# Second group of the first half's output contraction and the gate's second products, placed between the last chunk and the last heads' turns

## The chip, the cores and the metric

The kernel runs on one core of a Trainium2 chip. The metric is the device time of one execution in microseconds. TensorE is PE here, VectorE DVE, ScalarE ACT, GpSimd POOL; SP is the engine whose queue issues most loads.

## The reference, cut to what matters

Two layers over a sequence of 512 tokens with 1024 features. Layer 0 is an RWKV-7 time mixing with a SwiGLU FFN, layer 1 a differential attention with a SwiGLU FFN. The change lies at the end of the time mixing:

```python
_, y = lax.scan(step, state0, (r, decay, k, v, a, b))      # per head, 16 heads of 64
y = (y - mean) * rsqrt(var + LNX_EPS)                       # norm of each head
y = y * lnx_w + lnx_b + bonus
return (y * g) @ w_o                                        # g = sigmoid(xg @ g1) @ g2
...
x = x + rwkv7_time_mix(...)
h = rms_norm(x, g_ffn[0])
x = x + swiglu_ffn(h, w_gu, w_down)
```

## The kernel before, in words

Features lie on partitions, tokens along the free axis; weights and activations of most products are split into a high and a low part, so that one product is three matmuls (`mm3`, L156 to L158: high x high, high x low, low x high). The 16 heads are worked in two halves `w` of 8 heads, and each half's recurrence (`rec`) runs over 8 chunks of 64 tokens.

One chunk (`chunk`) is a chain between PE and DVE: products `L841` with V and the old state, a copy `L850` to SBUF, 16 small products `L855`, a copy `L860`, products `L841` with V and that copy, and the new state (`L868`, `L871`). The outputs of the chunk before (`chunk_y`, two groups of 24 small products `L883`, each copied by ACT in `L884`) are written between them. After two chunks a token tile of 128 is complete, and `head_out` makes its head norm: a first part (`L892` to `L899`, with the square `L896` on ACT), a second part (`L903` to `L914`: loads of V, the bonus on POOL, a root in ten small steps on DVE, the gain) and a third part, the turn to features on partitions: four transposes `L918` on PE and four copies `L921` on ACT into `oT`. `rec` runs these parts one or two chunks behind and drains them at its end.

`out_half(w)` closes a half. Its first step is the gate: `gate2` loads two tables (`g2a` through `L142`, `g2b` in three parts through `L436`), splits them (`L432`, `L433`, `L437`, `L438`) and makes four banks of four matmuls (three of `mm3` and `L443`); each bank is multiplied into `oT` and split (`ev`: `L650`, `L654`, `L656`). Then come two groups `gi` of four output tiles, each over the four feature tiles of the half: eight steps of 4 x 3 = 12 matmuls. Every second step loads 512 KB of `w_o` (`L142`), casts it on ACT (`L670`) and takes the low part on DVE (`L671`). When a group is done, `add` (`L662`) adds its banks to the residual `x1`.

`plan` writes the steps of three streams in an order by due times (`TIMES`): pairs, solve and recurrence of half 0; projections, gate and `out_half(0)`; pairs, solve and recurrence of half 1. A scheduler then orders each engine's queue by what it expects to be ready, and each engine works its queue in that order. So all of `out_half(0)` lies between the chunks of the second recurrence. `out_half(1)` is drained after the plan, behind `turn()`, which hands the space of the state tiles to the FFN. All weights share the tag `wr` with three buffers, for the raw tile and for the low part; PSUM banks are `ca` (2), `cb` (2) and `pj` (4). In the FFN `gain_split` (`L296`, `L297`) needs the finished residual.

Of the kernel before, what the change touches and what calls it, by code (L numbers as in the profile page):

```python
# [9 lines left out]
F32 = mybir.dt.float32  # L10
F32R = mybir.dt.float32r
BF = mybir.dt.bfloat16
AF = mybir.ActivationFunctionType
ALU = mybir.AluOpType
# [4 lines left out]
P = 128  # L19
# [23 lines left out]
class Trunk:  # L43
# [115 lines left out]

    def proj_k(self, W, x, evac, gi=0, banks=("pj",) * 4):  # L160


        pss = [self.bank(t) for t in banks]
        for kt in range(KT):
            if kt % 2 == 0:
                wh, wl = self.load_w(W[gi, kt // 2], [P, 2, 512])
            for i in range(4):
# [5 lines left out]

    def proj_f(self, W, xgen, evac, kts=range(KT), gi=0):

        pss = [self.bank() for _ in range(4)]
        for kt in kts:
            if kt % 2 == 0:
                w = self.load_raw(W[gi, kt // 2], [P, 2, 512])
            x = xgen(kt)  # L180
# [5 lines left out]

    def proj_p(self, W, xgen, evac, gi=0):

        nc = self.nc
        pss = [self.bank() for _ in range(4)]  # L190
        for kt in range(KT):
            if kt % 2 == 0:
                w = self.load_raw(W[gi, kt // 2], [P, 2, 512])
                wz, xz = (self.T("z", [P, 4, 512], F32R) for _ in range(2))
# [228 lines left out]
        nc.scalar.copy(self.low[:, 0, :], t)  # L423
        nc.vector.tensor_tensor(out=self.low[:, 1, :], in0=t, in1=self.low[:, 0, :].bitcast(F32), op=ALU.subtract)

    def gate2(self, pg, w, evac):

        nc, A = self.nc, self.A
        c0 = slice(w * 512, w * 512 + 512)
        raw = self.load_raw(A["g2a"][:, c0], [P, 512])  # L430
        hi, lo, st = (self.T("pr", [P, 512], F32R) for _ in range(3))
        nc.scalar.copy(hi, raw)  # L432
        nc.vector.tensor_tensor(out=lo, in0=raw, in1=hi.bitcast(F32), op=ALU.subtract)  # L433
        raw = self.T("wr", [P, 512])
        for i in range(3):
            nc.sync.dma_start(raw[i * 32:i * 32 + 32], A["g2b"][:, c0])  # L436
        nc.scalar.copy(st[0:96], raw[0:96])  # L437
        nc.vector.tensor_tensor(out=st[32:64], in0=raw[32:64], in1=st[32:64].bitcast(F32), op=ALU.subtract)  # L438
        for i in range(4):
            ps = self.bank()  # L440
            c = slice(i * P, i * P + P)
            self.mm3(ps, hi[:, c], lo[:, c], pg[0], pg[1], True, False)
            nc.tensor.matmul(ps, st[0:96, c], pg[2][0:96], start=False, stop=True)  # L443
            evac(w * 4 + i, ps)

    def rwkv(self, turn):
        nc, A = self.nc, self.A
        xT = self.h
        rstd = self.norm_cols(xT, "pr", True)
        bc = self.rows_bc(rstd, "pr")  # L450
        cp = self.cp
        self.omu = cp.tile([P, 6 * KT], F32, name="omu")
        i0 = VI["mu0"] * KT
        nc.vector.tensor_scalar(self.omu, self.par[:, i0:i0 + 6 * KT], -1.0, 1.0, op0=ALU.mult, op1=ALU.add)
        h = xT

        def normed():
            for j in range(KT):
                v = h[j // 2][:, j % 2, :]
                nc.vector.scalar_tensor_tensor(out=v, in0=v, scalar=self.vec("g_mix0", j), in1=bc, op0=ALU.mult, op1=ALU.mult)  # L460
                yield
        self.h = h
        self.Dc = cp.tile([P, NP, NCH], F32, name="Dc")
        self.bon = cp.tile([P, NT, NP, 2], F32, name="bon")
        self.rkc = cp.tile([P, NP, 2], F32, name="rkc")
        for p in range(NP):
            nc.vector.tensor_scalar(self.rkc[:, p, :], self.cst[:, C_BO:C_BO + 2], self.vec("r_k", p), None, op0=ALU.mult)
        self.lw = cp.tile([P, D], F32, name="lw")
        self.v_d = self.dr.tile([2, 2, S, 4, C], F32, name="v_d")
        self.st_d = self.dr.tile([2, NCH, P, 4, 8 * C], F32, name="st_d")  # L470
        self.sel = cp.tile([P, NT, P], F32, name="sel")
        self.R, self.Pt, self.kept = {}, {}, {}
        self.oT = {}

        self.merge(*zip((normed(), self.lora_h(h, "ca"), self.r_half(0)), self.START))
        sg, aa = self.rates(0)
        kr, ld, pg, sa, x1 = ([], []), ([], []), [], [(sg, aa)], []
        nc.gpsimd.dma_start(self.sel, A["sel"])
        self.drain(self.k_half(0, kr[0]))
        nc.sync.dma_start(self.lw, A["lnx_w"].broadcast_to([P, D]))  # L480

        def rates():
            sa.append(self.rates(1))
            yield

        def out(w):
            if w == 0:
                x1.extend(self.load_x())
            yield from self.out_half(w, pg, x1)
        t = self.TIMES  # L490
        self.plan(
            [(lambda: self.pairs(0, kr[0], *sa[0], ld[0]), 20, *t["pairs0"]), (lambda: self.solve(0, *ld[0]), 36, *t["solve0"]),
             (lambda: self.rec(0), 24, *t["rec0"])],
            [(lambda: self.r_half(1), 8, *t["r1"]), (lambda: self.k_half(1, kr[1]), 8, *t["k1"]), (rates, 1, t["k1"][1], t["k1"][1]),
             (lambda: self.v_half(0), 8, *t["v0"]), (lambda: self.v_half(1), 8, *t["v1"]), (lambda: self.gate(pg), 8, *t["gate"]),
             (lambda: out(0), 9, *t["out0"])],
            [(lambda: self.pairs(1, kr[1], *sa[1], ld[1]), 20, *t["pairs1"]), (lambda: self.solve(1, *ld[1]), 36, *t["solve1"]),
             (lambda: self.rec(1), 24, *t["rec1"])])
        turn()
        self.drain(out(1))  # L500
        return x1

    def mixes(self, key, m, w):
# [107 lines left out]
    def rec(self, w):  # L611
        for i in range(2):
            self.oT[w * 2 + i] = self.T("s", [P, 2, S])
        st, out, prev = None, [], ()
        nxt = self.chunk_load(w, 0)
        for c in range(NCH):
            cur, nxt = nxt, self.chunk_load(w, c + 1) if c < NCH - 1 else None
            if c % 2 == 0:
                y = self.T("ho", [P, 2, 4, C])
            fill = [self.chunk_y(*prev, par) for par in range(2)] if prev else []  # L620
            new, U = yield from self.chunk(w, c, st, *cur, fill)
            if c > 0 and c % 2 == 0:
                out.append(self.head_out(w, c // 2 - 1, prev[-1]))
            for g in out:
                next(g, None)
            out = out[-2:]
            prev = (c, st, U, *cur, y)
            st = new
        for par in range(2):
            next(self.chunk_y(*prev, par))  # L630
        out.append(self.head_out(w, NT - 1, y))
        for g in out:
            self.drain(g)

    def chunk_load(self, w, c):
        z = self.T("z", [P, 4, 8, C])
# [6 lines left out]
    def out_half(self, w, pg, x1):  # L643

        nc, A = self.nc, self.A
        yx, yh, yl = {}, {}, {}

        def ev(o, ps):
            yx[o] = self.T("xk", [P, S])
            nc.vector.tensor_tensor(out=yx[o], in0=ps, in1=self.oT[o // 2][:, o % 2, :], op=ALU.mult)  # L650
            if o % 2 == 0:
                yh[o // 2] = self.T("s", [P, 2, S], F32R)
            h = yh[o // 2][:, o % 2, :]
            nc.scalar.copy(h, yx[o])  # L654
            yl[o] = self.T("xk", [P, S], F32R)
            nc.vector.tensor_tensor(out=yl[o], in0=yx[o], in1=h.bitcast(F32), op=ALU.subtract)  # L656
        self.gate2(pg, w, ev)
        yield

        def add(o, ps):  # L660
            v = x1[o // 2][:, o % 2, :]
            nc.vector.tensor_tensor(out=v, in0=ps, in1=v, op=ALU.add)  # L662
        for gi in range(2):
            pss = [self.bank() for _ in range(4)]
            for kt in range(w * 4, w * 4 + 4):
                k = kt % 2
                if k == 0:
                    W = self.load_raw(A["w_o"][gi, kt // 2], [P, 2, 512])
                    wh, wl = self.T("s", [P, 2, 512], F32R), self.T("wr", [P, 2, 512], F32R)
                    nc.scalar.copy(wh, W)  # L670
                    nc.vector.tensor_tensor(out=wl, in0=W, in1=wh.bitcast(F32), op=ALU.subtract)  # L671
                for i in range(4):
                    c = slice(i * P, i * P + P)
                    self.mm3(pss[i], wh[:, k, c], wl[:, k, c], yh[kt // 2][:, k, :], yl[kt], k == 0 and kt % 4 == 0, kt % 4 == 3)
                    if kt % 4 == 3:
                        add(gi * 4 + i, pss[i])
                yield
# [613 lines left out]
```

## Time and profile before

| | us |
|---|---|
| runs (3) | 1504.1 median, 1504.0 to 1507.41 |
| the profiled execution | 1504.01, span 1502.2, mean granted clock 0.985 |
| PE busy | 1438.6 (96%) |
| DVE, ACT, POOL busy | 775.7, 514.0, 188.6 |
| HBM | 102 GB/s over the span |

A wait is put down to the instruction that came last. Durations of matmuls are modelled at their ends, so the spacing of their starts tells more than the mean of one. The views used are the busy shares, the table by stages, PE's waits, the chain of waits, the timeline, the groups of instructions and the list of loads.

### The profile page before, as it was taken

The numbers are of one execution on the slowest core, as the hardware profiler recorded it, in microseconds if no ns is written. First come the engines' busy times: TensorE is split into PE (matmuls) and PEld (weight loads), VectorE is DVE, ScalarE is ACT, GpSimd is POOL, SyncE is SP. The second block draws the span as 40 slices with busy tenths as digits, with TensorE's granted clock in tenths as the row PEclk, the third lists the DMA queues.
The fourth block names the chain that finished last, engine by engine and source line by source line (L and its number), as shares of the span: only waits on it lengthen the run. The fifth ranks groups of instructions, "written<-read, shape, count | busy, mean of one in ns | idle before, by whom it ended". The sixth has DMA issues, their size and how long they took to land.

```text
span 1502.2 us, 23112 instructions
## 1 busy us (share of the span) xinstructions
PE 1438.6 (96%) x9592; PEld 1142.1 (76%) x9592; DVE 775.7 (52%) x1497; ACT 514.0 (34%) x907; POOL 188.6 (13%) x156
## 2 busy tenths in 40 slices
PE   4999999999996999999999989999999999999998
PEld 2675555766885788888888889988778888888887
DVE  6625559588666643344323376666656444343222
ACT  4633242214323432233212253466654333222111
POOL 0013212101000211111100023110002111111000
PEclk9989999999998999999999999999999999999999
DMA  5203524766311322222222222211012222222231
GB/s 171 80 15 114 184 75 152 281 230 210 134 53 49 121 95 98 97 91 94 98 98 99 98 72 85 85 58 43 29 57 85 98 98 99 98 98 98 98 123 60
DMA packets 56761, 154.76 MB, mean 103 GB/s; under 512 B 10704, under 2 KB 17104, under 8 KB 54608
## 3 DMA queue, kind: packets, MB, share of 16 engines
q1 hardware_dynamic: 55456, 151.71, 29.4%
q8 instruction: 75, 1.23, 0.3%
q10 hardware_dynamic: 1120, 1.32, 0.3%
q14 instruction: 30, 0.25, 0.0%
q0 software_dynamic: 80, 0.26, 0.0%
HBM read 132.29 MB, written 20.97 MB: 102 GB/s over the span
## 4 chain that ended last, share of the span: by engine, by line
PE 83%; DVE 9%; ACT 3%; POOL 2%; issue 2%; DMA 1%; ACTq 0%; POOLq 0%
PE pj L156 15%; PE pj L157 15%; PE pj L158 15%; PE pj L182 3%; PE pj L216 3%; PE d L1067 2%; PE cb L883 2%; PE d L1069 2%; PE d L1068 2%; PE ca L841 2%; PE cb L751 1%; PE a L1165 1%; PE ca L157 1%; PE cb L157 1%; PE ca L156 1%
## 5 line engine op out<-in xcount | busy, mean ns | idle before, releaser
L150 ACT CAST wh<-wr 128x1024 fp32r<-128x1024 f32 x153 | 160.8, 1052 | 498.1 <-PE pj L157 217.5
L151 DVE TENSOR_TENSOR wl<-wr,wh 128x1024 fp32r<-128x1024 f32 x153 | 187.0, 1223 | 184.7 <-ACT wh L150 183.1
L156 PE MATMUL pj<-xa,wh 128*128 128x512 f32 x352 | 139.2, 395 | 1.3 <-ACT wh L150 1.3
L157 PE MATMUL pj<-xa,wh 128*128 128x512 f32 x352 | 138.9, 395 | 0.0
L158 PE MATMUL pj<-xa,wl 128*128 128x512 f32 x352 | 138.8, 395 | 0.0
L156 PE MATMUL pj<-xb,wh 128*128 128x512 f32 x352 | 137.1, 389 | 0.0
L158 PE MATMUL pj<-xb,wl 128*128 128x512 f32 x352 | 137.0, 389 | 0.0
L157 PE MATMUL pj<-xb,wh 128*128 128x512 f32 x352 | 136.9, 389 | 0.0
L954 POOL TENSOR_TENSOR hid<-ev,hid 128x512 fp32r<-128x512 f32 x44 | 68.2, 1551 | 403.6 <-ACT hid L953 403.6
L950 DVE TENSOR_TENSOR ev<-pj,bc 128x512 f32<-128x512 f32 x44 | 30.4, 691 | 144.0 <-PE pj L158 144.0
L947 DVE TENSOR_TENSOR ev<-pj,bc 128x512 f32<-128x512 f32 x44 | 30.4, 692 | 116.6 <-PE pj L158 114.3
L156 PEld LDWEIGHTS pj<-xa,wh 128*128 128x128 f32 x352 | 66.3, 188 | 17.5 <-ACT wh L150 2.2
L158 PEld LDWEIGHTS pj<-xa,wl 128*128 128x128 f32 x352 | 66.3, 188 | 15.6
L157 PEld LDWEIGHTS pj<-xa,wh 128*128 128x128 f32 x352 | 66.3, 188 | 15.2
L157 PEld LDWEIGHTS pj<-xb,wh 128*128 128x128 f32 x352 | 66.1, 188 | 13.8
L156 PEld LDWEIGHTS pj<-xb,wh 128*128 128x128 f32 x352 | 66.1, 188 | 13.7
L158 PEld LDWEIGHTS pj<-xb,wl 128*128 128x128 f32 x352 | 66.1, 188 | 13.5
L158 PE MATMUL pj<-hid,wl 128*128 128x512 f32 x176 | 68.5, 389 | 0.0
L156 PE MATMUL pj<-hid,wh 128*128 128x512 f32 x176 | 68.5, 389 | 0.0
L157 PE MATMUL pj<-hid,wh 128*128 128x512 f32 x176 | 68.5, 389 | 0.0
L216 PE MATMUL pj<-wr,xk 128*128 128x512 f32 x128 | 63.8, 637 | 0.0
L227 POOL TENSOR_TENSOR ty<-ty,mhalf 128x8 f32<-128x8 f32 (+1 forms) x20 | 35.4, 1769 | 156.6 <-DVE ty L1103 125.8
(342 smaller groups left out, 3096.7 us busy)
## 6 DMA issues: line engine op xcount, KB each, us to landing
wr<-in_wgu SPq DMA_DIRECT2D x88, 512.0 KB, 3.5
wr<-in_wdn SPq DMA_DIRECT2D x44, 512.0 KB, 3.5
st_d<-z SPq DMA_DIRECT2D x16, 1024.0 KB, 4.5
z<-st_d SPq DMA_DIRECT2D x16, 1024.0 KB, 5.6
wr<-in_w_kv SPq DMA_DIRECT2D x16, 512.0 KB, 3.6
wr<-in_w_r SPq DMA_DIRECT2D x8, 512.0 KB, 3.5
wr<-in_w_k SPq DMA_DIRECT2D x8, 512.0 KB, 3.4
wr<-in_w_v SPq DMA_DIRECT2D x8, 512.0 KB, 3.7
```

The source lines that it names most:

```text
L150: nc.scalar.copy(hi, raw)
L151: nc.vector.tensor_tensor(out=lo, in0=raw, in1=hi.bitcast(F32), op=ALU.subtract)
L156: mm(out, wh, xh, start=start, stop=False)
L157: mm(out, wh, xl, start=False, stop=False)
L158: mm(out, wl, xh, start=False, stop=stop)
L182: self.nc.tensor.matmul(pss[i], w[:, kt % 2, i * P:i * P + P], x, start=kt == kts[0], stop=kt == kts[-1])
L216: self.nc.tensor.matmul(pss[tt], x[:, tt * P:(tt + 1) * P], w[:, kt % 2, :], start=kt == 0, stop=kt == KT - 1)
L227: nc.gpsimd.tensor_tensor(out=y, in0=m, in1=half.to_broadcast(shp), op=ALU.pow)
L841: nc.tensor.matmul(ps[f, i * C:(i + 1) * C], L(f, i), R[f, i, :], start=False, stop=n == len(parts) - 1 and i == 3)
L947: nc.vector.tensor_tensor(out=a, in0=pss[0], in1=bc, op=ALU.mult)
L950: nc.vector.tensor_tensor(out=b, in0=pss[1], in1=bc, op=ALU.mult)
L954: nc.gpsimd.tensor_tensor(out=t[:, 1, :], in0=b, in1=t[:, 0, :].bitcast(F32), op=ALU.subtract)
```

## The change

Three things move. The second group (`gi` = 1) of `out_half(0)` leaves the plan: the plan now takes five steps of it (the gate and the first group), and the other four are drained after the plan. `rec` no longer drains the last head norm of the second half: its first two parts are written, and the turn is kept as `self.rest`. And `gate2` of the second half is cut in two: its products go to four banks `ca`, `ca`, `cb`, `pj` ahead of that turn, the multiplication `ev` comes after it; ahead of both, the first `w_o` tile of `out_half(1)` is loaded and split (`first`). `gate2` also makes all of its products before the first `ev`, in both halves. `turn()` comes after `out_half(1)`.

```diff
-    def gate2(self, pg, w, evac):
+    def gate2(self, pg, w, evac, banks=("pj",) * 4):
...
-        for i in range(4):
-            ps = self.bank()
+        pss = [self.bank(t) for t in banks]
+        for i, ps in enumerate(pss):
             c = slice(i * P, i * P + P)
             self.mm3(ps, hi[:, c], lo[:, c], pg[0], pg[1], True, False)
             nc.tensor.matmul(ps, st[0:96, c], pg[2][0:96], start=False, stop=True)
+        yield
+        for i, ps in enumerate(pss):
             evac(w * 4 + i, ps)
...
         t = self.TIMES
+        o0 = out(0)
         self.plan(
...
-             (lambda: out(0), 9, *t["out0"])],
+             (lambda: itertools.islice(o0, 5), 5, *t["out0"])],
...
+        o1 = out(1)
+        self.drain(o0)
+        next(o1)
+        self.drain(self.rest)
+        self.drain(o1)
         turn()
-        self.drain(out(1))
...
-        for g in out:
+        for g in out[:-1]:
             self.drain(g)
+        for _ in range(2):
+            next(out[-1])
+        if w:
+            self.rest = out[-1]
+        else:
+            self.drain(out[-1])
...
+        def split(gi, j):
+            W = self.load_raw(A["w_o"][gi, j], [P, 2, 512])
+            wh, wl = self.T("s", [P, 2, 512], F32R), self.T("wr", [P, 2, 512], F32R)
+            nc.scalar.copy(wh, W)
+            nc.vector.tensor_tensor(out=wl, in0=W, in1=wh.bitcast(F32), op=ALU.subtract)
+            return wh, wl
...
-        self.gate2(pg, w, ev)
+        if w:
+            first = split(0, 2)
+            yield from self.gate2(pg, w, ev, ("ca", "ca", "cb", "pj"))
+        else:
+            self.drain(self.gate2(pg, w, ev))
+            first = None
         yield
...
                 if k == 0:
-                    W = self.load_raw(A["w_o"][gi, kt // 2], [P, 2, 512])
-                    wh, wl = self.T("s", [P, 2, 512], F32R), self.T("wr", [P, 2, 512], F32R)
-                    nc.scalar.copy(wh, W)
-                    nc.vector.tensor_tensor(out=wl, in0=W, in1=wh.bitcast(F32), op=ALU.subtract)
+                    wh, wl = first or split(gi, kt // 2)
+                    first = None
```

The changed kernel's statements have other line numbers: `L650` becomes L670, `L654` L674, `L656` L676, `L662` L687, `L670` L664, `L671` L665, `L824` L847, `L841` L864, `L855` L878, `L883` L906, `L912` L935, `L914` L937, `L918` L941. The text goes by those of the kernel before.

On PE between two chunks of the second recurrence (chunk two in the kernel before), what stands between a chunk's last products and the next chunk's first; `pj` banks are the contraction's, `ca` the chunk's. Before:

```order
L841 MATMUL ca_614_3645<-rs_592_3474,z_591_3472 64x64 x8
L157 MATMUL pj_579_3417<-xk_570_3392,s_603_3564 128x512
L841 MATMUL ca_614_3645<-rs_613_3643,z_591_3472 64x64 x8
L158 MATMUL pj_579_3417<-s_566_3380,wr_604_3565 128x512
L156 MATMUL pj_580_3418<-s_566_3380,s_603_3564 128x512
L157 MATMUL pj_580_3418<-xk_570_3392,s_603_3564 128x512
L158 MATMUL pj_580_3418<-s_566_3380,wr_604_3565 128x512
L156 MATMUL pj_581_3419<-s_566_3380,s_603_3564 128x512
L157 MATMUL pj_581_3419<-xk_570_3392,s_603_3564 128x512
L158 MATMUL pj_581_3419<-s_566_3380,wr_604_3565 128x512
```

The same place now:

```order
L847 MATMUL ca_611_3615<-zero_77,cst_63 128x256
L864 MATMUL ca_611_3615<-rs_585_3452,z_584_3450 64x64 x8
L864 MATMUL ca_611_3615<-rs_610_3613,z_584_3450 64x64 x8
L156 MATMUL pj_590_3485<-s_562_3374,s_593_3489 128x512
L157 MATMUL pj_590_3485<-xk_565_3381,s_593_3489 128x512
L158 MATMUL pj_590_3485<-s_562_3374,wr_594_3490 128x512
L156 MATMUL pj_591_3486<-s_562_3374,s_593_3489 128x512
L157 MATMUL pj_591_3486<-xk_565_3381,s_593_3489 128x512
L158 MATMUL pj_591_3486<-s_562_3374,wr_594_3490 128x512
L847 LDWEIGHTS cst_63
L847 MATMUL ca_619_3663<-zero_77,cst_63 128x256
L864 MATMUL ca_619_3663<-rs_603_3552,z_602_3550 64x64 x8
```

Where twelve matmuls of the contraction stood around a chunk's last products, six stand now, and behind two other chunks none.

On PE around the last turn (`L918`, L941 in the changed kernel); `pr` tiles are the gate's table, `pj_732` and `pj_735` the second half's contraction. Before:

```order
L443 MATMUL pj_725_4390<-s_545_3322,pr_716_4360 128x512
L156 MATMUL pj_729_4401<-s_544_3321,pr_714_4358 128x512
L157 MATMUL pj_729_4401<-s_544_3321,pr_714_4358 128x512
L158 MATMUL pj_729_4401<-s_544_3321,pr_715_4359 128x512
L443 MATMUL pj_729_4401<-s_545_3322,pr_716_4360 128x512
L918 MATMUL cb_712_4343<-cst_63,ho_706_4314 128x128 x4
L156 MATMUL pj_732_4411<-s_720_4376,s_737_4417 128x512
```

Now:

```order
L157 MATMUL pj_723_4365<-s_544_3321,pr_716_4351 128x512
L941 MATMUL cb_724_4382<-cst_63,ho_696_4246 128x128 x4
L158 MATMUL ca_720_4362<-s_544_3321,pr_717_4352 128x512
L158 MATMUL ca_721_4363<-s_544_3321,pr_717_4352 128x512
L158 MATMUL cb_722_4364<-s_544_3321,pr_717_4352 128x512
L158 MATMUL pj_723_4365<-s_544_3321,pr_717_4352 128x512
L443 MATMUL ca_720_4362<-s_545_3322,pr_718_4353 128x512
L443 MATMUL ca_721_4363<-s_545_3322,pr_718_4353 128x512
L443 MATMUL cb_722_4364<-s_545_3322,pr_718_4353 128x512
L443 MATMUL pj_723_4365<-s_545_3322,pr_718_4353 128x512
L156 MATMUL pj_735_4413<-s_726_4393,s_713_4345 128x512
```

The 16 gate products stood ahead of the turn; now eight of them (those with the table's high part) and, ahead of these, the moved group of 48 stand before it, and the other eight behind it.

On DVE from the end of the last head norm to the gated tiles. Before:

```order
L908 TENSOR_TENSOR ho_675_4056<-ho_675_4056,ty_709_4324 128x512
L912 TENSOR_TENSOR ho_675_4056<-ho_675_4056,lw_157 128x256 x2
L914 TENSOR_TENSOR ho_706_4314<-ho_675_4056,ho_708_4319 128x4x64 x2
L650 TENSOR_TENSOR xk_719_4374<-pj_718_4369,s_571_3394 128x512
L656 TENSOR_TENSOR xk_721_4378<-xk_719_4374,s_720_4376 128x512
```

Now:

```order
L935 TENSOR_TENSOR ho_668_4006<-ho_668_4006,lw_157 128x256 x2
L937 TENSOR_TENSOR ho_696_4246<-ho_668_4006,ho_698_4251 128x4x64 x2
L687 TENSOR_TENSOR x_550_3335<-pj_702_4275,x_550_3335 128x512
L687 TENSOR_TENSOR x_550_3335<-pj_703_4276,x_550_3335 128x512
L687 TENSOR_TENSOR x_551_3337<-pj_704_4277,x_551_3337 128x512
L687 TENSOR_TENSOR x_551_3337<-pj_705_4278,x_551_3337 128x512
L433 TENSOR_TENSOR pr_717_4352<-wr_715_4349,pr_716_4351 128x512
L438 TENSOR_TENSOR pr_718_4353<-wr_719_4356,pr_718_4353 32x512
L670 TENSOR_TENSOR xk_725_4391<-ca_720_4362,s_571_3394 128x512
```

Four additions of the moved group and two steps of the gate's table have come between the norm's last step and the first gated tile. Further ahead, the split of the early `w_o` tile (`L671`, L665 now) stands among the small steps of the norm's root.

## Rows read from the trace of the kernel before

**Rows 1.** Busy time of PE, with its share of the span and its instructions.

```profile
PE 1438.6 (96%) x9592; PEld 1142.1 (76%) x9592; DVE 775.7 (52%) x1497; ACT 514.0 (34%) x907; POOL 188.6 (13%) x156
```

**Rows 2.** Table by stages: length; busy PE, PEld, DVE, ACT, POOL; clock; DMA share, GB/s.

```profile
470.00:493.00 23.00, 23.00 (x90) 18.46 (x91) 11.31 (x15) 6.32 (x8) 0.00 (x0) 0.89 0.26 91
...
380.00:452.40 72.40, 71.49 (x1074) 60.10 (x1073) 47.70 (x116) 16.98 (x36) 4.69 (x6) 1.00 0.26 86
452.40:469.90 17.50, 5.24 (x24) 3.83 (x23) 10.60 (x28) 5.95 (x14) 1.69 (x2) 0.76 0.14 45
```

**Rows 3.** PE's waits, 380 to 470 us: line waited for, us in total, times, longest.

```profile
PE pj L156 <- ACT s L670: 6.7, 1, 6.7
PE cb L918 <- DVE ho L914: 5.5, 1, 5.5
```

**Rows 4.** Chain of waits from the last chunks to the second contraction: start, us, what.

```profile
438.56 1.40 PE cb L883 x24
440.17 1.08 PE ca L841 x32
...
452.43 0.43 PE pj L157
...
456.10 0.53 ACT ho L896
456.65 0.70 DVE ty L898
...
462.10 1.10 PE cb L918 x4
463.22 1.14 ACT s L921 x4
464.36 0.61 ACT s L654
...
466.32 0.63 ACT s L654
...
469.91 0.79 PE pj L156
```

**Rows 5.** Timeline of PE in the second contraction: start, us, line, tiles.

```profile
475.31 0.40 PE L156 MATMUL pj<-s,s 128*128 128x512 f32 x1
...
478.05 0.39 PE L156 MATMUL pj<-s,s 128*128 128x512 f32 x1
...
492.33 0.39 PE L156 MATMUL pj<-s,s 128*128 128x512 f32 x1
...
494.14 0.39 PE L158 MATMUL pj<-s,wr 128*128 128x512 f32 x1
```

**Rows 6.** Groups of instructions, 376 to 500 us: busy us, mean ns, idle before.

```profile
L662 DVE TENSOR_TENSOR x<-pj,x 128x512 f32<-128x512 f32 x16 | 10.7, 688 | 6.5 <-PE pj L158 6.5
L671 DVE TENSOR_TENSOR wr<-wr,s 128x1024 fp32r<-128x1024 f32 x8 | 9.7, 1216 | 6.7 <-PE pj L158 5.2 <-ACT s L670 1.5
...
L650 DVE TENSOR_TENSOR xk<-pj,s 128x512 f32<-128x512 f32 x8 | 5.5, 685 | 2.3 <-ACT s L921 1.7 <-PE pj L443 0.6
...
L850 DVE COPY rs<-ca 128x256 f32<-128x256 f32 x7 | 2.9, 420 | 4.0 <-PE ca L841 4.0
...
L438 DVE TENSOR_TENSOR pr<-wr,pr 32x512 fp32r<-32x512 f32 x2 | 1.4, 681 | 0.1
...
L437 ACT CAST pr<-wr 96x512 fp32r<-96x512 f32 x2 | 1.2, 616 | 1.1 <-DMA wr<-in_g2b 1.1
```

**Rows 7.** Loads of the page: issues, KB each, median us from issue to landing.

```profile
wr<-in_g2a SPq DMA_DIRECT2D x2, 256.0 KB, 3.0
...
wr<-in_g2b SPq DMA_DIRECT2D x6, 64.0 KB, 2.8
```

**Rows 8.** Table by stages, columns as in rows 2, stretches of small products.

```profile
370.00:375.00 5.00, 4.76 (x27) 1.84 (x25) 4.59 (x17) 3.53 (x5) 0.45 (x1) 1.00 0.33 107
...
437.80:444.40 6.60, 6.60 (x136) 6.00 (x135) 3.57 (x8) 2.03 (x6) 0.34 (x1) 1.00 0.13 41
```

## Prediction

> **What bounds the kernel now.** I read the busy shares first. TensorE (PE) is busy 96% of the span [rows 1], so a change pays only where PE idles or runs at its lower clock; work that is merely moved from one full place to another pays nothing. The table by stages then says where it idles. From 380.0 to 452.4 us, the second recurrence with the first half's output contraction between its chunks, PE works 71.5 of 72.4 us. From 452.4 to 469.9 it works 5.2 of 17.5 us, at a mean granted clock of 0.76. From 470 to 493 it is full again, but at a mean clock of 0.89 [rows 2]. Two waits make nearly all of the hole: 5.5 us for the last `L914` and 6.7 us for the weight cast `L670` [rows 3]. The chain of waits shows what they hang on: the last chunk's `L883` ends at 452.43 (T0 below), then come the head norm on DVE and ACT, the turn `L918` at 462.10, `L921`, and the split of the gated tile (`L650`, `L654`, `L656`). The weight cast `L670` stands in ACT's queue behind the third `L654`, and only after it does the first product of the second half's contraction start, at 469.91 (S below) [rows 4]. S minus T0 is 17.5 us. The hole costs a second time: of the products behind it the first twelve take 5.40 us, from 469.91 to 475.31, about 0.45 each, which is the 1.2 GHz level; at the 2.4 GHz level they follow each other every 0.2267 us (63 steps from 478.05 to 492.33), and twelve take 2.72 [rows 4, 5]. So 2.7 us are lost to the clock. From S to the end of the 96 products (494.14 + 0.23) are 24.5 us.
>
> **The change part by part.** The profiled execution took 1504.01 us with a span of 1502.2; the median of the runs is 1504.1. I count from 1504.0.
>
> *Out of the recurrence.* The second group of the first half is 4 steps of 4 x 3 = 48 products, 48 x 0.2267 = 10.9 us. All of it leaves the stretch in which PE idles 0.9 us of 72.4 [rows 2], so it was on the path, and T0 comes 10.9 us earlier unless PE waits there instead. What it covered are the hand-overs of a chunk: PE ends a product, DVE copies it (`L850`, `L860`, 0.42 us each, or `L868` and `L871`, two such) and PE goes on with the copy. Around each of them the new order still has something: 24 products `L883` of the chunk before (1.40 us), 6 to 7 of the remaining large products, or the half of `L841` that needs no new state. A copy that comes at once (0.42 and some 0.2 for two semaphores) is covered by each of these. It is not where DVE does something else first: in the fourth chunk the copy now stands behind the last wide steps of a head norm (as wide as `L650`, 0.69), in the last behind a weight split `L671` (1.22) [rows 4, 6]. I put 0.3 and 0.4 us for the two. The trace of before has no chunk with so little fill, so the bounds are 0 and 2.4 us (both copies late by one whole `L671`); I stay near the lower end, because the 24 products cover most of either. T0: -10.9 + 0.7 = -10.2 us.
>
> *Into the hole.* After T0 PE's queue now holds 47 of the 48 moved products (10.65 us), the turn of the third token tile (0.55, half of the 1.10 that a turn took at the lower clock), 8 of the gate's 16 products (1.8), and only then the last `L918`: 13.0 us after T0. The head norm is ready before that. It took 9.7 us; `L896` now waits 0.5 us more behind the `L921` of the third tile, and a weight split `L671` (1.2) stands in the middle of its small DVE steps, 11.4 in all. So the norm is hidden and PE's own queue sets the turn. Behind the turn stands the gate: the four `L662` of the moved group, `L433` and `L438` go ahead of the first `L650` on DVE, and `L437` goes behind the last `L921` on ACT. From 13.0: turn 0.55, `L921` 1.14, `L437` 0.62, `L438` 0.68, the first `L443` 0.39, `L650` 0.69, `L654` 0.63, and some 0.5 for the semaphores between them, together 18.2 us after T0, against 17.5 before [rows 4 to 6]. The four `L662` and `L433` (as wide, 0.69) end at 11.4 + 5 x 0.69 = 14.9 and are not last. I take S as 0.8 us later after T0 than it was. The hole does not vanish, it is filled: four waits of 0.5 to 1 us stay in it.
>
> *The loads.* Three slots `wr` serve every weight. The gate's `g2a` can be loaded only when the `L671` of the early split is done: `L898` ends at T0 + 4.9, 0.5 later now, four small steps of 0.2 and the split follow, 7.4; it lands 3.0 us later, its cast (0.61, as `L437`) ends at T0 + 11.1, and PE asks for it at 11.2. `g2b` waits until PE has finished the moved group (T0 + 11.4); its third part is issued 0.9 later and there at 15.1, just when `L437` could read it [rows 4, 7]. I cost both at nothing; if either is late, each us of lateness is a us of the sum. Behind them on the SP queue stands the load of the next `w_o` tile, which is issued some 6 us before S and wanted 4 us after it. The loads of V, state and x stay ahead of these, as they were.
>
> *Second contraction.* Without the long idle time the clock should stay up, which gives back the 2.7 us. Against it: the cast `L670` of the second weight tile still stands behind three `L654`, which come every 1.96 us, so it ends at about S + 5.0, when 18 products (4.1 us) are done [rows 4]. I put 1.4 us for this and for the smaller waits of the next tiles, between 0 and 2.7. Gain 1.3 us.
>
> The sum: -10.2 + 0.8 - 1.3 = -10.7 us, so 1504.0 - 10.7 = **1493.3 us**. After the second contraction the order is as before, and all of it comes 10.7 us earlier.
>
> The Trainium skill, page "TensorE: Matmul & The Clock Gate", section "Back-to-back issue gap", gives about 131 ns as the sustained spacing of matmuls of 512 columns; by it the moved 48 would be 6.3 us and the sum 1497.9, an estimate. The rows show 0.2267 us over 63 steps [rows 5], so the measurement decides and the page's figure enters nothing.
>
> **The rivals.** *The loads come late.* Both gate loads pass through one slot each that is freed late. If that slips by one landing and one cast (3.0 + 0.6) and the recurrence by the rest of its bound (2.4 - 0.7), the sum is -10.7 + 5.3, 1498.6 at most; one of them alone gives 1495 to 1497. For it: both loads meet their reader within 0.2 us by my own count. Against it: landings of this size take about 3 us all through [rows 7].
>
> *The recurrence becomes bound by its hand-overs.* A chunk has three, about 0.6, 0.6 and 1.1 us, 2.3 in all, and seven chunks have them, 16 us. PE waited for hardly any of this before. If what is left covers only a third of it, 10.8 us come back and the change is a wash, 1504. For it: in two places a chunk and a half now pass without a large product. Against it: the groups of 24 products alone cover the first two hand-overs.
>
> *Slower: PE falls to its lower clock in the recurrence.* In those two places PE now has nothing but 64 x 64 products for over 8 us each (four groups `L883` of 1.40 and two and a half `L841` of 1.08) [rows 4]. At 1.2 GHz they would take twice as long, 17 us more, and the time would be 1510; it decides as soon as the granted clock in them reads well under 1.00. Against it: the trace has such a stretch of 6.6 us (437.8 to 444.4) at clock 1.00, and from 370 to 375, with PE's weight loads busy only 1.84 of 5 us, the clock reads 1.00 as well [rows 8]. The same page of the Trainium skill, section "Part 1: The HAM clock gate", says that the throttled state is the default and that activity releases it; no row here shows a recurrence with so few large products, so this keeps a small chance.
>
> That the change does not do what it says is no case of its own: the order shows the 48 products behind the last chunk.
>
> **How the numbers follow.** Forecast 0.75, with 1491 to 1496 of its own; late loads 0.12; bound by hand-overs 0.09; lower clock 0.04. Downward, a gate without waits (S 1 us nearer to T0) and a second contraction without them (1.4) give 1490.9. The range of 1490.5 to 1497.5 holds the forecast and most of the late loads. About 0.3% (4.5 us) is what a measurement here can tell from no change: faster by more than that 0.87, within it 0.09, slower 0.04.
>
> **What would show it.** In the new profile the last `L883` ends near 442.2; the last turn starts about 13 us after it and not 9.7; the wait for `L914` is gone, and small waits for `L433`, `L438` and `L654` stand in its place; the second contraction starts near 460.5, with steps of 0.23 us from the first, and ends near 483.7. The forecast is wrong if PE's waits for `L850`, `L860` and `L871` in the recurrence sum to over 3 us, if `L432` or `L437` waits long for its load, or if the clock reads under 1.00 before S.

## The result and the profile after

The changed kernel takes 1491.7 us (median of 4 runs, 1489.66 to 1492.96) against 1504.78 for the kernel before in the same series: ratio 0.9909, 95% interval [0.9894, 0.9924]. The forecast was 1493.3, range 1490.5 to 1497.5. The profiled execution took 1490.67 us, its span is 1488.9. Line numbers are each kernel's own from here on; in the changed kernel the chunk's products are `L864`, the copies behind them `L873` and `L883` (`L850` and `L860` before), and the second weight cast and split `L664` and `L665`.

PE's busy time, to set beside [rows 1]: 3.5 us less, all of it clock and spacing, since the instructions are the same 9592.

```profile
PE 1435.1 (96%) x9592; PEld 1138.8 (76%) x9592; DVE 774.2 (52%) x1497; ACT 513.9 (35%) x907; POOL 188.3 (13%) x156
```

The table by stages, cut at the same events as [rows 2] (the stretch up to T0, from T0 to S, the second contraction). Columns: stretch; length; busy PE, PEld, DVE, ACT, POOL; granted clock; DMA share, GB/s.

```profile
380.00:440.10 60.10, 59.20 (x1024) 50.14 (x1022) 41.85 (x107) 15.92 (x34) 4.73 (x5) 1.00 0.29 96
440.10:458.10 18.00, 16.11 (x73) 12.47 (x71) 12.36 (x31) 5.94 (x14) 1.85 (x3) 1.00 0.21 69
458.10:481.00 22.90, 22.35 (x95) 17.63 (x96) 14.80 (x21) 8.40 (x13) 0.00 (x0) 1.00 0.25 92
```

The recurrence is 12.3 us shorter, 0.6 of it ahead of its first chunk, and as full as it was (0.9 us idle in both). The hole is 0.5 us longer than it was, but PE now works 16.1 us of it and not 5.2. The clock reads 1.00 in all three, where the last two read 0.76 and 0.89 before.

PE's waits from 378 to 490 us: line waited for, us in total, times, longest. The waits of 5.5 and 6.7 us of [rows 3] are gone; what is left is under 1 us each, but for the first line: `L150` is the FFN's weight cast, and its wait is the same in the kernel before.

```profile
PE pj L156 <- ACT wh L150: 1.3, 2, 1.1
PE ca L864 <- DVE rs L883: 0.8, 1, 0.8
PE ca L443 <- DVE pr L438: 0.8, 1, 0.8
PE pj L156 <- ACT s L674: 0.7, 1, 0.7
PE pj L156 <- ACT s L664: 0.5, 1, 0.5
PE ca L158 <- DVE pr L433: 0.4, 1, 0.4
```

The chain of waits from the last chunk into the second contraction (start, us, what), beside [rows 4]:

```profile
438.63 1.54 PE cb L906 x24
440.16 0.43 PE pj L157
...
453.14 0.23 PE pj L157
453.37 0.45 PE cb L941 x4
453.84 0.70 ACT s L944 x3
...
454.98 0.50 ACT pr L437
455.51 0.69 DVE pr L438
456.25 0.51 PE ca L443
456.78 0.70 DVE xk L670
457.51 0.63 ACT s L674
...
462.08 0.95 ACT s L664
463.08 0.50 PE pj L156
```

From T0 to the turn (`L941`) the chain now runs on PE itself: the moved products, not the head norm, set the turn. Behind the turn stand the gate's second table (`L437`, `L438`, `L443`) and then the gated tile (`L670`, `L674`). The cast `L664` of the second weight tile still stands behind three `L674`, but no longer ahead of S: it costs PE 0.5 us inside the contraction.

**A yardstick for the experiments.** The differences looked for are a few us, and the stretch ahead of the second recurrence, where all kernels here have the same order, took 374.2 to 377.9 us in the profiled executions. So each trace is also measured between its own events: A is the start of the first chunk's copy on DVE in the second recurrence, T0 the start of what follows the last chunk's last small product on PE, S the first product of the second contraction, E the start of its last product plus one step (0.23). Each ratio is to the kernel before in the run's own series; its medians there were 1503.49 to 1505.13 us. In us:

| kernel | A | A to T0 | T0 to S | S to E | A to E | time, median | ratio to before, 95% |
|---|---|---|---|---|---|---|---|
| before | 375.50 | 76.86 | 17.55 | 24.46 | 118.87 | 1504.78 | 1 |
| changed | 374.88 | 65.22 | 18.08 | 23.05 | 106.35 | 1491.7 | 0.9909 [0.9894, 0.9924] |
| changed, again | 377.91 | 65.24 | 18.08 | 23.18 | 106.50 | 1493.01 | 0.9921 [0.9908, 0.9933] |
| moved group only | 374.57 | 65.22 | 20.17 | 24.29 | 109.68 | 1493.92 | 0.9941 [0.9928, 0.9953] |
| gate, turn, early tile only | 374.29 | 76.88 | 13.42 | 24.99 | 115.29 | 1501.67 | 0.9987 [0.9978, 0.9996] |
| before with dummies | 376.82 | 76.86 | 17.10 | 22.29 | 116.25 | 1502.48 | 0.9993 [0.9985, 1.0002] |
| both groups moved | 377.06 | 55.03 | 29.96 | 23.04 | 108.03 | 1495.68 | 0.9940 [0.9926, 0.9953] |
| tables ahead, turn first | 374.18 | 65.64 | 15.46 | 22.25 | 103.35 | 1488.12 | 0.9910 [0.9896, 0.9925] |
| the same again | 374.83 | 65.64 | 15.45 | 22.29 | 103.38 | 1487.01 | 0.9884 [0.9869, 0.9899] |
| tables ahead, turn last | 377.88 | 66.70 | 17.45 | 23.76 | 107.91 | 1492.89 | 0.9925 [0.9912, 0.9939] |
| turn first, tables late | 377.41 | 65.17 | 17.66 | 22.99 | 105.82 | 1492.7 | 0.9923 [0.9899, 0.9947] |
| tables ahead, no early tile | 374.58 | 65.67 | 19.22 | 24.28 | 109.17 | 1494.79 | 0.9941 [0.9919, 0.9963] |

Two traces of one kernel agree to 0.2 us in these columns, while A alone moves by 3 us. Where a median and A to E disagree by 1 or 2 us, this is why.

### The profile page after: what moved, and what is told of

Read it like the earlier page. It is cut to its first block, busy times and chain, and to the rows that moved or that the text cites. A ratio compares the mean times of both kernels' runs of the same rounds, so it can differ in the third digit from the quotient of the medians.

```text
span 1488.9 us, 23110 instructions
## 1 busy us (share of the span) xinstructions
PE 1435.1 (96%) x9592; PEld 1138.8 (76%) x9592; DVE 774.2 (52%) x1497; ACT 513.9 (35%) x907; POOL 188.3 (13%) x156
## 4 chain that ended last, share of the span: by engine, by line
PE 84%; DVE 8%; ACT 3%; POOL 2%; issue 2%; DMA 1%; SPq 0%; ACTq 0%; POOLq 0%
PE pj L156 15%; PE pj L157 15%; PE pj L158 15%; PE pj L182 3%; PE pj L216 3%; PE d L1090 3%; PE d L1092 2%; PE d L1091 2%; PE cb L906 2%; PE ca L864 2%; PE a L1188 2%; PE cb L774 2%; PE ca L157 1%; PE ca L156 1%; PE cb L157 1%
## 5 line engine op out<-in xcount | busy, mean ns | idle before, releaser
L150 ACT CAST wh<-wr 128x1024 fp32r<-128x1024 f32 x153 | 160.8, 1051 | 497.9 <-PE pj L157 224.2
```

## The experiments

**One half of the change alone, then the other.** First the moved group without the rest:

```diff
 # kernel before, with these two edits
+        o0 = out(0)
-             (lambda: out(0), 9, *t["out0"])],
+             (lambda: itertools.islice(o0, 5), 5, *t["out0"])],
...
+        self.drain(o0)
         turn()
         self.drain(out(1))
```

> Only the moved group: the second group of the first half's contraction (48 products) is drained behind the last chunk as in the changed kernel, but the last head norm, the gate and the second half's first weight tile are written as in the kernel before. T0 is the end of the last chunk's last small product, S the first product of the second contraction. My theory (three separate terms): T0 as early as in the changed kernel, 440 against 452.4; the turn (four transposes) about 10 us after T0, but the gate's 16 products all stand behind the moved group and the turn, and the weight cast stands behind three casts of gated tiles again, so S comes about 20 us after T0 instead of 18.0; the clock is full, steps of 0.23 us. Time 1493 to 1496. Rival 'the gate's rearrangement is worth nothing': S - T0 is 18, time 1491.7 as the changed kernel. Rival 'the move only pays together with the gate's rearrangement': over 1500.

Measured: 1493.92 us, and A to E 9.2 us shorter than before. T0 comes as early as in the changed kernel (A to T0 65.22 in both), S at T0 + 20.2 as expected. PE's waits from 384 to 490 us say why S is late: the weight cast is behind the gated tiles again.

```profile
PE pj L156 <- ACT s L672: 3.6, 1, 3.6
...
PE pj L158 <- DVE wr L673: 0.5, 1, 0.5
```

One thing was not expected: the clock does fall. The table by stages of this kernel, from the gate's last product on (idle, first three products, next nine), shows 0.52 in the third stretch:

```profile
455.96:459.96 4.00, 0.39 (x2) 0.00 (x0) 2.63 (x5) 2.18 (x3) 0.00 (x0) 1.00 0.00 0
459.96:461.47 1.51, 0.97 (x3) 0.49 (x3) 1.51 (x3) 1.15 (x2) 0.00 (x0) 0.97 0.04 11
461.47:464.94 3.47, 3.47 (x9) 2.75 (x9) 1.69 (x2) 0.42 (x1) 0.00 (x0) 0.52 0.19 51
```

So a single wait of 3.6 us costs its own length and 1.4 us more behind it: nine products take 3.47 us that take 2.04 at 0.2267. Then the other half:

```diff
 # changed kernel, with these two edits
-             (lambda: itertools.islice(o0, 5), 5, *t["out0"])],
+             (lambda: o0, 9, *t["out0"])],
...
-        self.drain(o0)
         next(o1)
```

> Only the other part: all nine steps of the first half's contraction stay between the chunks, while the last turn, the gate's products in four banks and the early first weight tile are as in the changed kernel. My theory: T0 stays near 452; the early weight tile takes the cast out of the chain (6.7 us of wait in the kernel before), so S comes 15 to 16 us after T0 instead of 17.5; the second contraction still begins at the lower clock, since TensorE has nothing to do for most of the hole. Time 1500 to 1503. Rival 'the gain is the gate's rearrangement': 1494 or less. Rival 'the early split in the norm eats what the cast gives': 1504.

Measured: 1501.67 us, A to E 3.6 us shorter. S comes at T0 + 13.4, two us earlier than I had worked out, since the weight cast is out of the way and the gate, as before, is done ahead of the turn; behind the turn PE waits only for the first gated tile, `L673` here (waits of PE, 384 to 490 us):

```profile
PE cb L940 <- DVE ho L936: 6.3, 1, 6.3
PE pj L156 <- ACT s L673: 1.8, 1, 1.8
```

But the long wait for the norm remains, PE works 5.4 us of the 13.5 us hole, and the contraction runs its first part at the lower clock (mean 0.88):

```profile
451.10:464.60 13.50, 5.39 (x27) 3.79 (x25) 8.35 (x27) 3.77 (x11) 1.19 (x2) 0.85 0.07 19
464.60:489.60 25.00, 25.00 (x96) 19.83 (x96) 15.02 (x21) 8.79 (x12) 0.00 (x0) 0.88 0.23 85
```

The two halves add up: 9.2 + 3.6 = 12.8 us against 12.4 to 12.5 for the whole. So the moved group is three quarters of the gain, and no rival stands: the rearrangement is neither worth nothing nor the whole gain, and the move pays without it. Inside the second half, only the early weight tile is taken out by itself (the last experiment); the four banks and the later `turn()` have no run of their own.

**The clock alone.** The kernel before, with 36 products behind the last chunk and 14 behind the gate whose result nobody reads:

```diff
+    def dummy(self, x, n):
+        ps = self.bank("ca")
+        for _ in range(n):
+            self.nc.tensor.matmul(ps, x[:, 0:P], x, start=True, stop=True)
...
+        self.dummy(pg[0], 36)
         turn()
         self.drain(out(1))
...
         self.gate2(pg, w, ev)
+        if w:
+            self.dummy(pg[0], 14)
```

> The kernel before, with nothing moved, and 50 products added whose result nobody reads: 36 behind the last chunk and 14 behind the gate, so that TensorE works through most of the hole. It measures the clock's share by itself. My theory: T0 stays at 452, S - T0 at 16.5 to 17.5 (the turn takes 0.55 instead of 1.10), the second contraction starts with steps of 0.23 us instead of 0.45, its end comes 2 to 3 us earlier; time 1501 to 1502.3. Rival 'the contraction is paced by the gated tiles, the clock hides behind them': 1504, with waits in place of slow steps. Rival 'filling the hole is most of the gain, whatever fills it': 1496 or less.

Measured: 1502.48 us, an interval that touches no change; between its own events 2.6 us less, of it 0.45 in the hole (the turn at full clock) and 2.17 in the contraction. In the table by stages the hole is full and the contraction reads 1.00 and not 0.89:

```profile
453.60:470.70 17.10, 16.33 (x76) 12.86 (x74) 10.53 (x28) 5.93 (x14) 1.40 (x2) 1.00 0.16 47
470.70:493.00 22.30, 22.22 (x96) 17.79 (x96) 12.62 (x17) 7.33 (x11) 0.00 (x0) 1.00 0.29 94
```

Filling a hole with just anything gives back the clock and no more. The Trainium skill, page "TensorE: Matmul & The Clock Gate", section "Part 1: The HAM clock gate", says that the throttled state is the default and that activity releases it; this trace agrees, since with products that serve nothing in the hole the clock behind it reads 1.00 and not 0.89.

**How much cover the recurrence needs.** The changed kernel, with the first group moved as well:

```diff
-             (lambda: itertools.islice(o0, 5), 5, *t["out0"])],
+             (lambda: itertools.islice(o0, 1), 1, *t["out0"])],
```

> The changed kernel with the first group of the first half's contraction moved as well: no large product of the contraction is left between the chunks of the second recurrence, all 96 stand behind the last chunk. X0 is where this stretch begins (387 to 390 us), E the end of the second contraction; X0 to E is 93.5 us in the changed kernel. My theory: the small products cover the hand-overs nearly alone, TensorE's waits for the chunk's copies grow by 1 to 3 us, the granted clock stays 1.00, T0 comes another 8 to 10 us earlier, and as the hole was already full the moved products now push the turn and S back by as much (the gate's waits are covered, 0 to 2 us gained): within 2 us of the changed kernel, 1490 to 1494. Rival 'hand-overs bind as soon as the large products are gone': waits of 8 to 16 us in the recurrence, 1497 to 1505. Rival 'the clock falls in a recurrence of small products alone': clock well under 1.00 before T0 and 1500 or more.

Measured: 1495.68 us. A to T0 is another 10.2 us shorter. Not all 96 products stand behind the last chunk, as I had written: the scheduler places nine of them ahead of it, the first at 418.40 us. So 40 fewer large products stand ahead of T0 than in the changed kernel; by their spacing they took 10.7 us (13.5 against 2.8). From 397.9 to 418.3 us no product of 512 columns runs at all. PE's waits in the whole recurrence (380 to 432 us) are one line:

```profile
PE cb L906 <- DVE rs L883: 0.4, 1, 0.4
```

The table by stages has the recurrence, the stretch of small products alone inside it, the hole and the second contraction; the clock reads 1.00 in the first two:

```profile
380.00:432.00 52.00, 51.54 (x1003) 44.36 (x995) 38.64 (x104) 16.37 (x36) 4.36 (x6) 1.00 0.29 92
397.90:418.30 20.40, 20.33 (x459) 18.77 (x458) 18.07 (x56) 7.37 (x16) 3.17 (x4) 1.00 0.25 71
432.00:462.00 30.00, 26.73 (x114) 21.03 (x112) 17.22 (x37) 7.12 (x15) 2.22 (x2) 0.94 0.24 77
462.00:485.00 23.00, 22.48 (x96) 17.63 (x96) 14.94 (x21) 8.60 (x12) 0.00 (x0) 1.00 0.28 92
```

Both rivals about the recurrence fall: in the 20.4 us without a large product the small ones cover its hand-overs by themselves (0.07 us idle), and the clock stays up. The time was still above the 1490 to 1494 that I expected, and A to E is 1.5 to 1.7 us over the changed kernel, because the first rival of the prediction shows itself here, the late loads. In the chain of this kernel the `w_o` tile of the moved group lands late, its split frees the slot for `g2a` late, and PE waits 2.4 us for the table. Behind this wait the clock falls as well, hence the 0.94 of the hole:

```profile
446.07 3.46 DMA wr<-in_w_o
...
449.55 1.06 ACT s L664
...
450.64 1.24 DVE wr L665
...
451.89 2.58 DMA wr<-in_g2a
...
454.49 0.63 ACT pr L432
...
455.16 0.50 PE ca L156
```

**Filling what is left of the hole.** The chain of the changed kernel has the gate's second table on the path behind the turn, and the turn behind half of the gate. Both can go: the tables are loaded and split ahead of the moved group, and the turn stands directly behind it, so that its copies run beside the gate's 16 products.

```diff
     # gate2: stop once behind the tables
+        yield
         pss = [self.bank(t) for t in banks]
...
         o1 = out(1)
-        self.drain(o0)
         next(o1)
+        self.drain(o0)
         self.drain(self.rest)
...
+            g = self.gate2(pg, w, ev, ("ca", "ca", "cb", "pj"))
+            yield next(g)
             first = split(0, 2)
-            yield from self.gate2(pg, w, ev, ("ca", "ca", "cb", "pj"))
+            yield from g
```

> The changed kernel with another order in the hole: the gate's two tables are loaded and split ahead of the moved group (during the recurrence), the last turn stands directly behind the moved group, and the gate's 16 products behind the turn, beside the copies of the turned tiles. My theory: in the changed kernel the chain from the turn to S (18.0 us after T0) holds two splits of the table and their products (0.62, 0.68, 0.39 us and what lies between); off the chain, the turn comes at T0 + 11.5 instead of 13.0 and S at T0 + 15.5 to 16, with TensorE hardly waiting: 2 to 2.5 us faster than the changed kernel, 1489 to 1490. Rival 'the gated tiles pace the start of the second contraction': S comes earlier but waits between its steps give it back, 1491.5. Rival 'the tables' splits now hold up the last chunks': T0 later by 1 to 3 us, 1491 to 1494.

Measured: 1488.12 us, and once more, in one series with the changed kernel:

> Tables ahead and the turn directly behind the moved group, the same kernel again, beside the changed kernel on one chip: my theory from its trace (X0 to E 90.5 against 93.5 us) is 3 us less than the changed kernel; if the difference of the first runs was scatter, none.

> The changed kernel itself, as the yardstick of this series: X0 to E 93.5 us again, and 12 to 13 us less than the kernel before.

1487.01 us (1486.81 to 1487.31) against 1493.01 (1490.55 to 1495.32). Between A and E the difference is 3.0 to 3.1 us in each pair of traces, and the fastest runs of all are 1486.81 and 1489.66; 2 to 2.5 us were expected. The rest of the 6 us between the medians lies ahead of A, where both kernels have the same order (A is 374.83 here and 377.91 there). In the first series, which had no run of the changed kernel, the ratio of 0.9910 is no better than the changed kernel's 0.9909, and two of its five runs took 1492 us; the gain rests on the second series and on the traces. In this kernel's table by stages (second series) PE works all 37.8 us from the last chunk to the end of the second contraction:

```profile
388.00:440.40 52.40, 52.15 (x909) 44.34 (x907) 37.88 (x98) 13.89 (x31) 4.00 (x5) 1.00 0.34 109
440.40:456.00 15.60, 15.60 (x75) 12.73 (x73) 11.77 (x31) 4.84 (x12) 1.81 (x3) 1.00 0.17 50
456.00:478.20 22.20, 22.20 (x97) 17.65 (x95) 14.25 (x20) 8.61 (x12) 0.00 (x0) 1.00 0.28 95
```

The rival that the tables' splits hold up the chunks has a little to it: A to T0 is 0.4 us longer. Which of the two edits did it? With the tables ahead but the turn behind the gate (`next(o1)` once more ahead of `self.drain(self.rest)`):

> The tables are loaded and split ahead of the moved group, as in the experiment before it that did this, but the last turn stands behind all 16 gate products. It tells apart what that experiment's gain is due to. If the place of the turn decides: the turn waits in TensorE's queue until 63 products are done (T0 + 14.5), S comes at T0 + 17.9, 2.4 us later than there, 1490 to 1491.5. If the early tables alone decide (no waits for their splits): S at T0 + 15.5, 1488.

With the turn first but the tables where the change has them (`self.drain(self.rest)` ahead of `next(o1)` in the changed kernel):

> The changed kernel with the last turn directly behind the moved group, ahead of all 16 gate products, but with the gate's tables loaded and split where they are in the changed kernel. Together with the two runs that have the tables ahead it gives all four combinations. My theory: the turn comes 1.8 us earlier (T0 + 11.3), but the gate's first tile still waits for the split of the second table (T0 + 15.4 in the changed kernel) and its product, so S stays at T0 + 17.5 to 18.1 and T0 to E at 40.5 to 41.2, within 0.6 us of the changed kernel. Rival 'the turn's place alone decides': S at T0 + 15.5, 3 us faster than the changed kernel.

T0 to E is 41.2 us with the turn late, 40.65 with the tables late (as expected), 41.1 to 41.3 in the changed kernel, and 37.7 only with both. Either edit alone meets the other's wait. Turn late, PE waits for the gated tile (`L676`), and the clock falls with that; tables late, for their splits (`L433`, `L438`), then for the gated tile (`L674`), then for the second weight tile (`L664`). PE's waits of the first and of the second, 384 to 500 us:

```profile
PE pj L156 <- ACT s L676: 1.8, 1, 1.8
```

```profile
PE pj L156 <- ACT s L674: 0.7, 1, 0.7
PE pj L156 <- ACT s L664: 0.4, 1, 0.4
PE ca L443 <- DVE pr L438: 0.4, 1, 0.4
PE ca L158 <- DVE pr L433: 0.4, 1, 0.4
```

The expected 1488 or 1490 to 1491.5 for the late turn was missed by over 1 us: I had priced S (T0 + 17.9, measured 17.45) but not the clock behind it. Its A to T0 is 1.1 us longer than its twin's with the same order up to T0; its trace has the clock at 0.79 from 380 to 388 us, ahead of the contraction's first product, which the other traces don't have. Why it fell there stays open.

Last, the early weight tile by itself, taken out of the best kernel:

```diff
-            first = split(0, 2)
+            first = None
```

> Tables ahead and turn directly behind the moved group as in the best kernel so far, but the second half's first weight tile is not split early: its cast stands again behind the casts of the gated tiles on ScalarE. It prices that part of the change by itself. My theory: S waits for the cast behind three gated tiles, T0 + 19 to 20 instead of 15.5, and the clock falls in that idle time, so T0 to E is 41 to 43 us instead of 37.7: 3.5 to 5.5 us slower than with the early tile. Rival 'the cast only moved the wait elsewhere': the products wait for the gated tiles anyway, at most 1 us slower.

Measured: 1494.79 us, A to E 5.8 us longer, a little above the expected 3.5 to 5.5. PE's waits show the cast ahead of S again, and its split behind it; the mean clock from 460 to 485 us is 0.93.

```profile
PE pj L156 <- ACT s L665: 3.6, 1, 3.6
...
PE pj L158 <- DVE wr L666: 0.5, 1, 0.5
```

## Why the prediction was right, and where its terms were off

The forecast held, at 1493.3 for 1491.7, and for the reasons given; three terms had another size.

**Out of the recurrence: -10.2 foreseen, -11.6 measured (A to T0).** The 48 products gave what they take: from the first product of the first half's contraction to T0 the spacings of the large products sum to 24.4 us before (97 products, one of the second half's gate among them) and to 13.5 now (49). The step that failed is the +0.7 for two late copies. The copies were late, as written: here is DVE in the last chunk (timeline: start, us, line), where the copy `L873` starts only when the split `L665` is done.

```profile
433.35 1.22 DVE L665 TENSOR_TENSOR wr<-wr,s 128x1024 fp32r<-128x1024 f32 x1
434.49 0.41 DVE L873 COPY rs<-ca 128x256 f32<-128x256 f32 x1
```

But it ends at 434.90, and PE has small products `L906` until 435.39 and no wait there; the only wait of the recurrence is `L883`, 0.8 us, and the kernel before had the same one. I had the cover in hand (24 products, 1.40 us) and still charged 0.7 us of the lateness; the run with both groups moved, 0.4 us of waits in 52 us, shows that the cover would have carried more. The other 0.7 us lie in the spacing of the small products (some 0.5) and in the two turns that fall into the recurrence (1.14 to 0.87 us by their spacing). Why the small ones became closer I did not follow up; it stays open.

**Into the hole: +0.8 foreseen, +0.5 measured.** The terms of the prediction make 0.7 (18.2 less 17.5), not 0.8. The turn was put at T0 + 13.0 and came at 13.1; PE's own queue sets it. The order of waits behind it is the one forecast: `L437`, `L438`, `L443`, the gated tile. The loads were costed at nothing, rightly: `L432` ended at 451.02, T0 + 10.9 (11.1 foreseen), and PE asked for the table at T0 + 11.3. That margin of 0.4 us was real and thin; with the first group moved as well it became a wait of 2.4 us.

**Second contraction: -1.3 foreseen, -1.3 to -1.4 measured,** as the difference of two terms that were each too large, so that the agreement is in part luck. The clock gives 2.2 us there and not 2.7 (the dummies: S to E from 24.46 to 22.29; another 0.45 comes in the hole, in the turn). The waits cost 0.8 and not 1.4 (23.05 against the dummies' 22.29).

**The rivals.** Late loads: not here, but a mechanism of this kernel, as seen with both groups moved. Bound by hand-overs: refuted, with both groups moved 0.07 us idle in the 20.4 us without a large product. Lower clock in the recurrence: refuted, 1.00 throughout in the changed kernel and with both groups moved.

**What the prediction did not see.** It gave the gate's rearrangement and the early tile no price of their own; its term for the hole, +0.8, looks as if they gave nothing. Without them the moved group gives 9.2 us and not 12.5, since the cast returns to the path and with it the lower clock. Nor did the prediction ask what the best order of the hole would be; its own list of what stands behind the turn contained the answer.

The terms together: A to E -12.5, another -0.6 ahead of A, which is within the scatter of A, and -0.2 behind E make the 13.3 us between the two profiled executions.

## What to carry to other kernels

An engine's full stretch next to its idle stretch is an invitation to move independent work, and the work moved is worth its full spacing as long as what stays behind covers the hand-overs; count that cover in the engine's own queue before charging a late producer. In a hole that is being filled, list what stands between the last input and the first product that is needed, and take each of it off the chain: two edits that are worth next to nothing singly (0.0 and 0.5 us here, T0 to E) were worth 3.5 together (3.0 to 3.1 from A, since the early tables cost 0.4 ahead of T0), because each was covered by the other's wait. And measure between events of the trace, not only by the whole time, where the rest of the kernel scatters by more than the effect.

## What the runs showed of the hardware

The granted clock did not fall during a wait of 3.6 us but after it: two kernels with that wait (the moved group alone, and the best kernel without the early tile) ran their first three products 0.23 to 0.34 us apart, waited 0.55 us once more and only then fell to 0.43 us per product for some 3 us. It also fell behind shorter waits, of 2.4 us with both groups moved and of 1.8 us with the turn late. Waits of 0.4 to 0.8 us in a row, four within 10 us in the changed kernel, left it at 1.00.

With both groups moved the clock read 1.00 through a recurrence of 52 us that is nearly all products of 64 x 64, with 20.4 us in which no product of 512 columns runs; I had given a small chance to the contrary.

A switch from small products to large ones costs PE about 0.1 us: in these traces the first large product behind small ones is followed after 0.34 us and not after 0.23, as in the timeline of the changed kernel (start, us, line):

```profile
396.14 0.50 PE L156 MATMUL pj<-s,s 128*128 128x512 f32 x1
396.48 0.39 PE L157 MATMUL pj<-xk,s 128*128 128x512 f32 x1
396.71 0.40 PE L158 MATMUL pj<-s,wr 128*128 128x512 f32 x1
```

At the 2.4 GHz level the large products followed each other every 0.23 us, at the 1.2 GHz level every 0.43, in all traces. The Trainium skill, page "TensorE: Matmul & The Clock Gate", section "Part 1: The HAM clock gate", gives 215.7 and 426.7 ns for 512 columns; the slow one agrees, the fast one measures 5% more here (0.2267 us, [rows 5]).
